# A hybrid decoder layer on one core: the mixer's first projection on x·g·(1 + scale), with the norm's roots multiplied into its sums

## The chip, the cores and the metric

The kernel runs on one core of a Trainium2 chip. The core has a matrix engine (TensorE, "PE" in the profile, with its weight loads as "PEld"), a vector engine (VectorE, "DVE"), an activation engine (ScalarE, "ACT"), a general engine (GpSimd, "POOL"), and a queue that issues transfers from device memory (SyncE, "SP"). Each engine runs its own instructions in order; they wait for each other through semaphores. The metric is the device time of one execution in microseconds, the median of several runs.

## The reference

One layer on x of 256 tokens by 2048 features: a feed-forward block at half weight, a token mixer, a second feed-forward block, a final norm. Ahead of each of the three blocks stands the same modulated norm, whose shift and scale (like the gate behind the block) come from a conditioning vector c.

```python
def rmsnorm(x, g):
    y = xf * lax.rsqrt(jnp.mean(xf * xf, axis=-1, keepdims=True) + EPS)
    return y * g
def ada_in(x, g, shift, scale):
    return rmsnorm(x, g) * (1.0 + scale[:, None, :]) + shift[:, None, :]

cond = jax.nn.silu(c)
mod = cond @ ada_w[l] + ada_b[l]          # 9 x 2048 values
sh1, sc1, gt1, sh2, sc2, gt2, sh3, sc3, gt3 = jnp.split(mod, 9, axis=-1)
h = ada_in(x, norm_g[l, 0], sh1, sc1)
x = x + 0.5 * gt1 * swiglu(h, w_gate0, w_up0, w_down0)
h = ada_in(x, norm_g[l, 1], sh2, sc2)
x = x + gt2 * hybrid_mixer(h, w_in, w_out, ...)
h = ada_in(x, norm_g[l, 2], sh3, sc3)
x = x + 0.5 * gt3 * swiglu(h, w_gate1, w_up1, w_down1)
return rmsnorm(x, final_norm)
```

`hybrid_mixer` projects h by `w_in` (queries, keys and values of 8 attention heads; queries, keys and values of 8 delta-rule heads behind a causal convolution of 4 taps and a silu; 24 gate columns; an output gate z), runs both groups of heads, and projects by `w_out`.

## The kernel before

**Layout.** Features lie on the 128 partitions, tokens along the free axis: x is 16 slices (index j or k, `KD` = 16) of 128 features by 256 tokens. A weight matrix is cut into tiles of 128 by 128; 5392 of them are packed in the order of use into 674 blocks of 8.

**Weights.** `Stream.next` (L124) hands out tiles. For each block it issues one transfer of 512 KB into a `wraw` tile (L119), ScalarE rounds it to `whi` (L121), VectorE makes the rest `wlo` = `wraw` - `whi` (L133). Four tiles of each kind exist (a few more of `wraw` in the feed-forward blocks), so a block's `whi` and `wlo` wait until TensorE has used the block four before. Activations are split the same way into `hs` HI and LO, and a product is hi·hi + hi·lo + lo·hi, three matrix instructions of 256 columns (L758 to L760 in the mixer), or one of 512 and one of 256 (L482, L483).

**Modulation columns.** The 144 columns of `mod` (9 parts of 16) are each a 1 MB transfer `adat` (L253) and one VectorE instruction over 2048 elements (L257). They are strewn between the weight blocks at the rate that `RATE` gives: from block 168 on 0.38 columns a block, from 264 on 0.1, from 280 on 0.25, from 408 on 0.125.

**Blocks by stage.** The first feed-forward block takes weight blocks 0 to 263; its last part, the down-projection of the second half, takes 232 to 263, two blocks for each of its 16 output slices j. The mixer's input projections are blocks 264 to 377, its output projection 378 to 409; the second feed-forward block is 410 to 673.

**Between the first feed-forward block and the mixer.** For each slice j of the down-projection, `residual` (L506, L507) adds to x on VectorE, `sumsq_add` squares on ScalarE (L306) and adds up on GpSimd (L310). Then `mixer` calls `modulate`: `norm_sums` (L320 on TensorE, L325 on ScalarE, L326 to L330 on VectorE) makes the inverse roots, `norm_row` (L338, L339) lays them out as a row over the tokens, and `modulate_one` makes h for one slice: x·g(1 + scale)·root (L365), plus shift and rounding to HI on ScalarE (L367, L368, L372), LO on VectorE (L369, L373). The projections begin with these h.

**The first projection** (`project`, L749) runs four outputs together, the slice k outside and the four inside: the gate columns ("gt") and the keys of heads 0 to 2; 8 blocks, 264 to 271. `gates` (L788) and `conv_silu` (L904) read its sums. Then come K3 to K7, single key heads of two blocks each, Z0 and V0 (z and attention values, 8 blocks each), and then G and F steps, which hold the heads' own work. `tick` advances that work (`gates`, `keys`, `solve`, `gdn`, `fox`) as the projections proceed; a scheduler then places each engine's instructions, and PSUM banks come from three pools of 3, 3 and 2.

**The second feed-forward block** begins in another way, by the class `Early`: `y(j)` writes x·g(1 + scale), without root and shift, into `hs` as soon as slice j of the output projection is done (L405 HI on ScalarE, L406 LO on VectorE), with the shift as one more column behind each half (258 columns at L421 and L423). `step(k)` makes the roots while the first products run, and the true h behind them; `scaled` (L427 to L430) multiplies the finished sums by the root row and takes out the shift's sum, which the reader adds as a bias.

Of the kernel before, what the change touches and what calls it, by code (L numbers as in the profile page):

```python
# [32 lines left out]

RATE = ((0, 0.5), (24, 0.34), (56, 0.45), (68, 0.06), (112, 0.5), (168, 0.38), (264, 0.1), (280, 0.25), (408, 0.125))
N_BIG, N_GDN = 3, 3
# [111 lines left out]
def layer_kernel(ctx: ExitStack, tc: tile.TileContext, xrow, c, adaw, cols, cst, w, out, order, dbg=None):  # L147
# [203 lines left out]

    plain = hsf[:, : KD * HS].rearrange("p (k i) -> p k i", k=KD)[:, :, : 2 * T].rearrange("p k (q t) -> p k q t", q=2)

    def part(k, q, extra=0):
# [5 lines left out]

    def modulate_one(j, g1, sh, r, weave=True):

        t = pt("ht")
        hl, hh, tt = (run(j, LO), run(j, HI), turns(t)) if weave else (plain[:, j, LO], plain[:, j, HI], t)
        V.scalar_tensor_tensor(t, x[:, j], g1, r, ALU.mult, ALU.mult)  # L365
        if j % 2:
            A.activation(t, t, AF.Identity, bias=sh)  # L367
            A.copy(hh, tt)  # L368
            return V.tensor_tensor(hl, tt, hh.bitcast(F32), ALU.subtract)  # L369
        else:  # L370
            with tc.issue_after(W.cast) if W.first else nullcontext():
                A.activation(hh, tt, AF.Identity, bias=sh)  # L372
            return V.scalar_tensor_tensor(hl, tt, sh, hh.bitcast(F32), ALU.add, ALU.subtract)  # L373
# [7 lines left out]

    def modulate(which, m_sh, m_sc):
        ada_need(max(m_sh, m_sc), KD - 1)
        g1 = gains(which, m_sc, 0, KD)
        r = norm_row(norm_sums())
        hq["next"], hq["one"] = 0, lambda j: modulate_one(
            j, g1[:, j : j + 1], mod[:, m_sh * KD + j : m_sh * KD + j + 1], r, False)

    class Early:

        def __init__(self, which, m_sh, m_sc):
            self.which, self.m_sh, self.m_sc, self.row, self.rstd = which, m_sh, m_sc, None, None

        def y(self, j):
# [7 lines left out]
            g = gains(self.which, self.m_sc, j, 1)  # L404
            A.activation(run(j, HI), turns(x[:, j]), AF.Copy, scale=g)  # L405
            V.scalar_tensor_tensor(run(j, LO), turns(x[:, j]), g, run(j, HI).bitcast(F32), ALU.mult, ALU.subtract)  # L406

        def step(self, k):
# [3 lines left out]
            if k == 4:  # L412
                self.row = norm_row(self.rstd, A.copy)
                g1 = gains(self.which, self.m_sc, 0, KD)
                hq["next"], hq["one"] = 0, lambda j: modulate_one(
                    j, g1[:, j : j + 1], mod[:, self.m_sh * KD + j : self.m_sh * KD + j + 1], self.row)
            if k > 4:
# [7 lines left out]
        def scaled(self, dst, ps):  # L425
# [3 lines left out]
            V.tensor_add(s[:, 1:], ps[:, T + 1 : T + 2], s[:, :1])  # L429
            V.tensor_tensor(dst, ps[:, :T], self.row, ALU.mult)  # L430
            return s[:, 1:]
# [180 lines left out]
    def ffn(which, m_gt, early=None):  # L612
        fs = list(range(NF))
        with tc.tile_pool(name=f"hid{which}", bufs=PARTS[which][1] + HIDX) as hp, \
                tc.tile_pool(name=f"more{which}", bufs=1) as more:
            W.more = more if MORE else None
            for half in range(2):
# [5 lines left out]
                for j in range(KD):  # L623
# [87 lines left out]
    early.close()  # L711
    norm2 = Early(2, 6, 7)
    if dbg is None or "ffn1" in dbg:
# [4 lines left out]
    def mixer():  # L718
        modulate(1, 3, 4)
        mx = ExitStack()  # L720
# [27 lines left out]

        def project(items):  # L749

            pp = [psn(i, "pp") for i in range(len(items))]
            todo = [(i, k) for k in range(KD) for i in range(len(items))]
            for i, k in todo:
                m, n = items[i]
                h_need(k)
                wh, wl = W.next(m, k, n)
                hh, hl = woven(plain[:, k, HI]), woven(plain[:, k, LO])
                PE.matmul(pp[i][:, :T], wh, hh, start=(k == 0), stop=False)  # L758
                PE.matmul(pp[i][:, :T], wh, hl, start=False, stop=False)  # L759
                PE.matmul(pp[i][:, :T], wl, hh, start=False, stop=(k == KD - 1))  # L760
                tick(TILE_US)
            return [p_[:, :T] for p_ in pp]

        def project_rows(mat, grp):

            pv = [psb("pv0"), psb("pv1")]
            for k in range(KD):
                wh, wl = W.next(mat, k, 4 * grp, 4)
                for t in range(2):
                    hh, hl = (plain[:, k, q, t * P : (t + 1) * P] for q in (HI, LO))  # L770
                    PE.matmul(pv[t], hh, wh, start=(k == 0), stop=False)
# [131 lines left out]

        def conv_silu(ps, n, dst):  # L904
# [4 lines left out]
            for s in range(1, 4):  # L909
                V.scalar_tensor_tensor(cv[:, s:], cp[:, : T - s], tap(3 - s), cv[:, s:], ALU.mult, ALU.add)  # L910
            A.activation(dst, cv, AF.Silu)
# [271 lines left out]

        def have_keys(h, ps):
            kk[h] = otile("kk")
            conv_silu(ps, NH + h, kk[h].bitcast(F32)[:, 0])
            if h % 4 == 0:
# [47 lines left out]
        W.late = True  # L1235
        first = project([("gt", 0)] + [("qkv", NH + h) for h in range(3)])
        start("k", -1, gates(first[0]))
        for h in range(3):
            have_keys(h, first[1 + h])
        for name in ORDER:  # L1240
# [183 lines left out]
```

## Time and profile before

| what | value |
|---|---|
| median of 3 runs | 1952.88 us (1949.29 to 1954.36) |
| the profiled execution | 1954.36 us |
| its span, first to last instruction | 1952.6 us |
| mean granted TensorE clock | 0.993 |
| weight and other transfers | 519.58 MB, mean 266 GB/s |

The profiled execution is the slowest of the three runs; its span is 1.8 us shorter than its device time. The page gives busy times by engine, the span in slices, the chain of waits that ended last, and groups of instructions by line; the trace gives every instruction in order of time. Matrix instructions are pipelined: one of 256 columns is shown with 0.28 us but the next one starts 0.11 us later, so the pace of TensorE is read from starts.

### The profile page before, as it was taken

What the parts mean: (1) busy time and instruction counts of PE and PEld (TensorE: products, weight loads), DVE (VectorE), ACT (ScalarE), POOL (GpSimd) and SP (SyncE); (2) the same over time, 40 slices, a digit from 0 to 9 for tenths busy, and PEclk for the clock granted to TensorE, in tenths of its full rate; (3) what the DMA queues carried; (4) which work ended last, traced back from release to release, by engine and by line L of the source; (5) the groups of instructions that cost most, each with busy time, mean ns of one, the idle gap of its engine ahead of it and who ended that gap; (6) DMA issues with size and microseconds to landing.
All of it is one profiled execution on the core that took longest, in us unless ns stands there. A gap on an engine that the chain in (4) does not pass through costs nothing.

```text
span 1952.6 us, 33709 instructions
## 1 busy us (share of the span) xinstructions
PE 1902.9 (97%) x13087; PEld 1776.3 (91%) x13087; DVE 1557.3 (80%) x2415; ACT 1035.5 (53%) x1645; POOL 57.0 (3%) x55
## 2 busy tenths in 40 slices
PE   8999999999999999999999999999999999999998
PEld 6999999998999988889989998889999999999997
DVE  6999978989999997889978979886766656565654
ACT  6544554433454446857657655565554445555553
POOL 0000000000000120000000002000000000000011
PEclk8999999999999999999999999999999999999999
DMA  9989867999999986685566658676777665555553
GB/s 369 359 321 349 300 221 254 398 381 376 356 353 342 347 317 218 251 302 205 203 239 236 211 215 315 226 258 249 255 249 239 201 200 203 201 200 202 200 202 119
DMA packets 129490, 519.58 MB, mean 266 GB/s; under 512 B 18217, under 2 KB 21545, under 8 KB 111153
## 3 DMA queue, kind: packets, MB, share of 16 engines
q1 hardware_dynamic: 129330, 517.42, 72.7%
q8 instruction: 103, 1.69, 0.3%
q14 instruction: 57, 0.47, 0.1%
HBM read 512.89 MB, written 4.47 MB: 265 GB/s over the span
## 4 chain that ended last, share of the span: by engine, by line
PE 76%; DVE 11%; DMA 5%; issue 4%; ACT 3%; SPq 0%; DVEq 0%; ACTq 0%
PE pd L482 14%; PE pg L478 10%; PE pu L478 10%; PE pd L483 7%; PE pu L479 5%; PE pg L479 5%; PE pgu L566 5%; PE pgu L565 5%; PE pgu L564 5%; DVE wlo L133 4%; DMA adat<-in_ada_dram 3%; DVE adat L257 2%; PE pp L758 2%; PE pp L759 2%; PE pp L760 2%
## 5 line engine op out<-in xcount | busy, mean ns | idle before, releaser
L133 DVE TENSOR_TENSOR wlo<-wraw,whi 128x1024 fp32r<-128x1024 f32 x674 | 821.1, 1227 | 242.7 <-ACT whi L121 241.3
L121 ACT CAST whi<-wraw 128x1024 fp32r<-128x1024 f32 x674 | 700.1, 1047 | 509.3 <-PE pd L482 166.5
L482 PE MATMUL pd<-hid,whi 128*128 128x512 f32 x1408 | 461.8, 382 | 0.0
L483 PE MATMUL pd<-hid,wlo 128*128 128x256 f32 x1408 | 384.6, 273 | 2.6 <-DVE wlo L133 2.4
L257 DVE CUSTOM_DVE_ANT_0 adat<-adat,cs,colt 128x2048 f32<-128x2048 f32 x140 | 329.5, 2354 | 40.9 <-DMA adat<-in_ada_dram 40.8
L478 PE MATMUL pg<-hs,whi 128*128 128x512 f32 x912 | 302.1, 382 | 2.5 <-DVE shc L429 2.5
L478 PE MATMUL pu<-hs,whi 128*128 128x512 f32 x912 | 302.2, 382 | 0.0
L482 PEld LDWEIGHTS pd<-hid,whi 128*128 128x128 f32 x1408 | 266.0, 189 | 36.5
L483 PEld LDWEIGHTS pd<-hid,wlo 128*128 128x128 f32 x1408 | 270.3, 192 | 5.4 <-DVE wlo L133 5.3
L564 PE MATMUL pgu<-hs,whi 128*128 128x256 f32 x896 | 245.3, 277 | 6.2 <-ACT hs L368 6.2
L479 PE MATMUL pu<-hs,wlo 128*128 128x256 f32 x912 | 249.3, 273 | 0.0
L479 PE MATMUL pg<-hs,wlo 128*128 128x256 f32 x912 | 248.9, 273 | 0.0
L566 PE MATMUL pgu<-hs,wlo 128*128 128x256 f32 x896 | 245.2, 278 | 2.4 <-DVE wlo L133 2.4
L565 PE MATMUL pgu<-hs,whi 128*128 128x256 f32 x896 | 246.8, 277 | 0.0
L478 PEld LDWEIGHTS pg<-hs,whi 128*128 128x128 f32 x912 | 172.4, 189 | 26.7 <-ACT whi L121 2.7
L478 PEld LDWEIGHTS pu<-hs,whi 128*128 128x128 f32 x912 | 172.4, 189 | 23.7
L758 PE MATMUL pp<-hs,whi 128*128 128x256 f32 x656 | 188.9, 289 | 1.5 <-ACT hs L372 1.5
L760 PE MATMUL pp<-hs,wlo 128*128 128x256 f32 x656 | 182.7, 278 | 1.1 <-DVE wlo L133 1.1
L759 PE MATMUL pp<-hs,whi 128*128 128x256 f32 x656 | 182.5, 278 | 0.0
L564 PEld LDWEIGHTS pgu<-hs,whi 128*128 128x128 f32 x896 | 172.3, 193 | 6.9 <-ACT hs L368 6.6
L479 PEld LDWEIGHTS pu<-hs,wlo 128*128 128x128 f32 x912 | 175.0, 192 | 1.3 <-DVE wlo L133 1.2
L479 PEld LDWEIGHTS pg<-hs,wlo 128*128 128x128 f32 x912 | 175.1, 192 | 0.4
(337 smaller groups left out, 2583.6 us busy)
## 6 DMA issues: line engine op xcount, KB each, us to landing
wraw<-in_w_dram SPq DMA_DIRECT2D x674, 512.0 KB, 4.3
adat<-in_ada_dram SPq DMA_DIRECT2D x140, 1024.0 KB, 7.4
xr<-in_xr_dram SPq DMA_DIRECT2D x4, 512.0 KB, 5.1
adaf<-in_ada_dram SPq DMA_DIRECT2D x4, 512.0 KB, 8.7
adaf<-in_ada_dram SPq DMA_DIRECT2D x2, 1024.0 KB, 11.3
xd<-x SPq DMA_DIRECT2D x4, 512.0 KB, 5.0
rw<-rowd SPq DMA_DIRECT2D x16, 128.0 KB, 6.7
x<-xd SPq DMA_DIRECT2D x4, 512.0 KB, 5.4
```

Of the source, the lines that this page charges most:

```text
L121: self.cast = self.nc.scalar.copy(self.h, r).ins
L133: nc.vector.tensor_tensor(self.l, r, self.h.bitcast(F32), ALU.subtract)
L257: V.tensor_tensor_reduce(t, t, cs, 1.0, L("adab", q, 1), ALU.mult, ALU.add, mod[:, q : q + 1])
L478: PE.matmul(ps, wt[0], both, start=(k == 0), stop=False)
L479: PE.matmul(ps[:, T:], wt[1], part(k, HI), start=False, stop=(k == KD - 1))
L482: PE.matmul(ps, wt[0], act.rearrange("p q (a b) -> p q b a", a=2), start=first, stop=False)
L483: PE.matmul(ps[:, :T], wt[1], woven(act[:, 0]), start=False, stop=last)
L564: PE.matmul(o, wh, part(k, HI), start=first and s == 0, stop=False, skip_group_check=skip)
L565: PE.matmul(o, wh, part(k, LO), start=False, stop=False, skip_group_check=skip)
L566: PE.matmul(o, wl, part(k, HI), start=False, stop=last, skip_group_check=skip)
L758: PE.matmul(pp[i][:, :T], wh, hh, start=(k == 0), stop=False)
L760: PE.matmul(pp[i][:, :T], wl, hh, start=False, stop=(k == KD - 1))
```

## The change

The mixer's first projection gets the treatment that the second feed-forward block has.

- `Early` takes a `view`, how the tokens of a slice are read: `turns` as so far, `runs` for the mixer. `norm1` is made for the mixer, and `norm1.y(j)` runs in the first feed-forward block's last down-projection behind each slice j. `modulate` is gone.
- The first `project` call gets `norm1`: 258, 256 and 258 columns on y; `early.step(k)` makes the roots at k = 2 and the root row at k = 4, and h for the later projections behind it. `conv_silu` of heads 0 to 2 and `gates` read their sums through `scaled`.
- `hs` keeps one layout, two halves of 128 tokens with 16 spare columns each, through the mixer; the matrix instructions read 256 columns in the same turn as before.
- `RATE` from block 232 on: 0.24, none from 264, 0.31 from 288, none from 404, 0.125 from 424.

```diff
-RATE = ((0, 0.5), (24, 0.34), (56, 0.45), (68, 0.06), (112, 0.5), (168, 0.38), (264, 0.1), (280, 0.25), (408, 0.125))
+RATE = ((0, 0.5), (24, 0.34), (56, 0.45), (68, 0.06), (112, 0.5), (168, 0.38), (232, 0.24), (264, 0.0), (288, 0.31), (404, 0.0), (424, 0.125))
...
-            A.activation(run(j, HI), turns(x[:, j]), AF.Copy, scale=g)
-            V.scalar_tensor_tensor(run(j, LO), turns(x[:, j]), g, run(j, HI).bitcast(F32), ALU.mult, ALU.subtract)
+            A.activation(run(j, HI), self.view(x[:, j]), AF.Copy, scale=g)
+            V.scalar_tensor_tensor(run(j, LO), self.view(x[:, j]), g, run(j, HI).bitcast(F32), ALU.mult, ALU.subtract)
...
-            V.tensor_tensor(dst, ps[:, :T], self.row, ALU.mult)
+            if self.view is turns:
+                V.tensor_tensor(dst, ps[:, :T], self.row, ALU.mult)
+            else:
+                V.tensor_tensor(runs(dst), turns(ps[:, :T]), runs(self.row), ALU.mult)
...
-                        if which == 1:
+                        if which == 0:
+                            norm1.y(j)
+                        else:
...
-    norm2 = Early(2, 6, 7)
+    norm1, norm2 = Early(1, 3, 4, runs), Early(2, 6, 7, turns)
...
     def mixer():
-        modulate(1, 3, 4)
...
-        def project(items):
+        def project(items, early=None):
...
+                if early is not None:
+                    if i == 0:
+                        early.step(k)
+                    early.products(pp[i], W.next(m, k, n), k)
+                    continue
...
+            if early is not None:
+                h_upto(KD)
+                return pp
...
-            A.copy(runs(yr[R]), turns(ps[R]))
+            d = pt("ey")
+            s = norm1.scaled(d, ps)
+            A.activation(yr[R], d[R], AF.Identity, bias=s[R])
...
-            A.copy(runs(cp), turns(ps))
+            if early is None:
+                A.copy(runs(cp), turns(ps))
+            else:
+                s = early.scaled(cp, ps)
+                A.activation(cp, cp, AF.Identity, bias=s)
...
-        first = project([("gt", 0)] + [("qkv", NH + h) for h in range(3)])
+        first = project([("gt", 0)] + [("qkv", NH + h) for h in range(3)], norm1)
```

The table of rates moves columns as follows, counted in the order of the transfers: 11 become 7 in blocks 232 to 263, 3 become none in 264 to 289, 29 become 36 in 290 to 404, 4 become none in 405 to 428, 10 become 14 behind.

**TensorE at the start of the mixer.** `pd_` are the sums of the last down-projection, `pp_` those of the first projection, one number for each bank in use. Before:

```order
L482 MATMUL pd_8153<-hid_7339,whi_8178 128x512
L483 MATMUL pd_8153<-hid_7339,wlo_8180 128x256
L320 MATMUL nsum_8209<-colt_87,sqacc_7394 128x2 x2
L320 MATMUL nsum_8209<-colt_87,sq_8202 128x2 x2
L339 MATMUL nrow_8224<-colt_87,rb_8223 128x128 x2
L758 MATMUL pp_8277<-hs_127,whi_8301 128x256
```

And now:

```order
L477 MATMUL pd_8203<-hid_7339,whi_8228 128x512
L478 MATMUL pd_8203<-hid_7339,wlo_8230 128x256
L413 MATMUL pp_8309<-hs_127,whi_8315 128x258
L414 MATMUL pp_8309<-hs_127,whi_8315 128x256
L415 MATMUL pp_8309<-hs_127,wlo_8317 128x258
L413 MATMUL pp_8310<-hs_127,whi_8315 128x258
```

The sums of squares (`nsum`) have moved behind the first block of products, 24 matrix instructions later, and the root row (`nrow`) into the third block; the products follow the down-projection directly.

**VectorE at the end of the first projection.** Before, where `cv_` is a convolution's sum and `ht_` a slice of h in the making:

```order
L369 TENSOR_TENSOR hs_127<-ht_8528,hs_127 128x256
L133 TENSOR_TENSOR wlo_8625<-wraw_8621,whi_8623 128x1024
L257 ISA adat_8627,mod_126<-adat_8627,cs_86,colt_87 128x2048
L257 ISA mod_126 128x1
L133 TENSOR_TENSOR wlo_8661<-wraw_8657,whi_8659 128x1024
L133 TENSOR_TENSOR wlo_8730<-wraw_8726,whi_8728 128x1024
L795 TENSOR_SCALAR coef_8639<-coef_8639 128x24
```

And now, where `pp_8310` and `pp_8311` are the sums of key heads 0 and 1, whose banks K3 and K4 take over:

```order
L363 SCALAR_TENSOR_TENSOR ht_8644<-x_85,g1_8395,nrow_8393 128x256
L133 TENSOR_TENSOR wlo_8693<-wraw_8689,whi_8691 128x1024
L367 TENSOR_TENSOR hs_127<-ht_8605,hs_127 128x2x128
L133 TENSOR_TENSOR wlo_8732<-wraw_8728,whi_8730 128x1024
L371 SCALAR_TENSOR_TENSOR hs_127<-ht_8628,mod_126,hs_127 128x2x128
L421 TENSOR_TENSOR shc_8652<-pp_8310,shc_8652 128x1
L425 TENSOR_TENSOR cp_8650<-pp_8310,nrow_8393 128x256
L421 TENSOR_TENSOR shc_8665<-pp_8311,shc_8665 128x1
```

The product of head 0's sums with the root row (L425), which releases the bank, stands on VectorE behind all but one of the instructions that make h and behind both blocks of K3; the modulation column has left. The gate columns' product comes three blocks of `wlo` behind this place.

**VectorE at the start of the second feed-forward block**, behind the root row's two instructions (L338). Before:

```order
L338 TENSOR_SCALAR rb_14473<-colt_87,nstd_14422 128x128 x2
L133 TENSOR_TENSOR wlo_14556<-wraw_14552,whi_14554 128x1024
L257 ISA adat_14666,mod_126<-adat_14666,cs_86,colt_87 128x2048
L257 ISA mod_126 128x1
L365 SCALAR_TENSOR_TENSOR ht_14507<-x_85,g1_14481,nrow_14479 128x256
```

And now:

```order
L338 TENSOR_SCALAR rb_14552<-colt_87,nstd_14501 128x128 x2
L133 TENSOR_TENSOR wlo_14635<-wraw_14631,whi_14633 128x1024
L133 TENSOR_TENSOR wlo_14674<-wraw_14670,whi_14672 128x1024
L363 SCALAR_TENSOR_TENSOR ht_14586<-x_85,g1_14560,nrow_14558 128x256
L363 SCALAR_TENSOR_TENSOR ht_14614<-x_85,g1_14560,nrow_14558 128x256
```

The modulation column between the root row and the making of h is gone, and one more block of weights stands there.

More of the change, by code (lines that the diff above doesn't have):

```diff
@@ L359, in run, with modulate_one @@
         return hs[:, k, q, :, :P]
-    def modulate_one(j, g1, sh, r, weave=True):
+    def modulate_one(j, g1, sh, r, view=turns):
         t = pt("ht")
-        hl, hh, tt = (run(j, LO), run(j, HI), turns(t)) if weave else (plain[:, j, LO], plain[:, j, HI], t)
+        hl, hh, tt = run(j, LO), run(j, HI), view(t)
         V.scalar_tensor_tensor(t, x[:, j], g1, r, ALU.mult, ALU.mult)
@@ L380, in gains, with __init__ @@
         return g1
[L382 to L387, printed above, removed]
     class Early:
-        def __init__(self, which, m_sh, m_sc):
+        def __init__(self, which, m_sh, m_sc, view):
             self.which, self.m_sh, self.m_sc, self.row, self.rstd = which, m_sh, m_sc, None, None
+            self.view = view
         def y(self, j):
@@ L415, in step @@
                 hq["next"], hq["one"] = 0, lambda j: modulate_one(
-                    j, g1[:, j : j + 1], mod[:, self.m_sh * KD + j : self.m_sh * KD + j + 1], self.row)
+                    j, g1[:, j : j + 1], mod[:, self.m_sh * KD + j : self.m_sh * KD + j + 1], self.row, self.view)
             if k > 4:
@@ L769, in project_rows @@
                 for t in range(2):
-                    hh, hl = (plain[:, k, q, t * P : (t + 1) * P] for q in (HI, LO))
+                    hh, hl = (hs[:, k, q, t, :P] for q in (HI, LO))
                     PE.matmul(pv[t], hh, wh, start=(k == 0), stop=False)
@@ L902, in mixer, with conv_silu @@
             G.memset(t_, 0.0)
-        def conv_silu(ps, n, dst):
+        def conv_silu(ps, n, dst, early=None):
             cp, cv = pt("cp"), pt("cv")
             tap = lambda s: L("conv", 4 * n + s, 1)
-            A.copy(runs(cp), turns(ps))
+            if early is None:
[3 more added lines that the diff above has]
+                A.activation(cp, cp, AF.Identity, bias=s)
             A.activation(cv, cp, AF.Copy, scale=tap(3))
-            for s in range(1, 4):
-                V.scalar_tensor_tensor(cv[:, s:], cp[:, : T - s], tap(3 - s), cv[:, s:], ALU.mult, ALU.add)
+            for d in range(1, 4):
+                V.scalar_tensor_tensor(cv[:, d:], cp[:, : T - d], tap(3 - d), cv[:, d:], ALU.mult, ALU.add)
             A.activation(dst, cv, AF.Silu)
@@ L1235, in mixer @@
         W.late = True
-        first = project([("gt", 0)] + [("qkv", NH + h) for h in range(3)])
+        first = project([("gt", 0)] + [("qkv", NH + h) for h in range(3)], norm1)
         start("k", -1, gates(first[0]))
         for h in range(3):
-            have_keys(h, first[1 + h])
+            have_keys(h, first[1 + h], norm1)
         for name in ORDER:
```

7 lines of the change are left out of this document (3 added, 4 removed).

## Prediction

> **What bounds the kernel now.** I read the page's totals and chain first, then busy times by stage (the windows view), then each engine's timeline at the edited places.
>
> ```profile
> span 1952.6 us, 33709 instructions
> PE 1902.9 (97%) x13087; PEld 1776.3 (91%) x13087; DVE 1557.3 (80%) x2415; ACT 1035.5 (53%) x1645; POOL 57.0 (3%) x55
> PE 76%; DVE 11%; DMA 5%; issue 4%; ACT 3%; SPq 0%; DVEq 0%; ACTq 0%
> ```
>
> TensorE sets the end: it is busy for 97%, and only 49.7 us are its holes. The change removes no large product, so it can save only holes, a low clock, or waits. Windows (start:end and length; busy time with count for PE, PEld, DVE, ACT, POOL; granted clock; DMA share; GB/s):
>
> ```profile
> 660.00:742.00 82.00, 81.07 (x493) 73.87 (x491) 74.25 (x95) 37.70 (x49) 21.83 (x15) 1.00 0.84 318
> 742.00:748.00 6.00, 1.66 (x10) 1.35 (x10) 5.46 (x15) 2.26 (x6) 1.07 (x5) 0.86 0.53 184
> 748.00:754.00 6.00, 6.00 (x33) 6.00 (x33) 5.22 (x12) 3.12 (x8) 0.42 (x2) 0.57 0.20 78
> 858.00:872.00 14.00, 9.98 (x83) 9.23 (x81) 12.43 (x20) 13.91 (x34) 0.43 (x2) 1.00 0.96 339
> 872.00:1000.00 128.00, 122.23 (x982) 116.38 (x981) 113.85 (x329) 84.34 (x208) 0.00 (x0) 1.00 0.59 205
> 1000.00:1050.00 50.00, 49.60 (x330) 46.02 (x330) 38.48 (x50) 29.35 (x42) 0.00 (x0) 1.00 0.81 298
> 1050.00:1150.00 100.00, 96.85 (x827) 93.83 (x826) 86.06 (x220) 64.78 (x155) 0.00 (x0) 1.00 0.55 198
> 1277.00:1280.00 3.00, 0.47 (x4) 0.47 (x4) 3.00 (x10) 2.18 (x8) 0.00 (x0) 1.00 1.00 403
> ```
>
> Four places matter: the step into the mixer (742 to 754: 4.34 us idle, then granted clock 0.57); the down-projection ahead of it, where VectorE is busy for 91% of the time; the mixer from 858 on, where TensorE loses 4.02 + 5.77 + 0.40 + 3.15 = 13.3 us; and the start of the second feed-forward block (2.53 us idle at 1277).
>
> **A, the step into the mixer.** TensorE's rows before (start, duration, instruction, in brackets what it waited for):
>
> ```profile
> 741.42 0.27 PE L483 MATMUL pd<-hid,wlo 128*128 128x256 f32 x1
> 741.53 0.51 PE L320 MATMUL nsum<-colt,sqacc 128*128 128x2 f32 x4
> 747.69 1.23 PE L758 MATMUL pp<-hs,whi 128*128 128x256 f32 x4 [1.55 <-ACT hs L372]
> 752.54 0.42 PE L759 MATMUL pp<-hs,whi 128*128 128x256 f32 x1
> 752.76 0.42 PE L760 MATMUL pp<-hs,wlo 128*128 128x256 f32 x1
> 771.73 0.28 PE L760 MATMUL pp<-hs,wlo 128*128 128x256 f32 x1
> 771.84 0.28 PE L758 MATMUL pp<-hs,whi 128*128 128x256 f32 x1
> ```
>
> Call 741.53 t0. The first product comes 6.2 us later, at half pace (0.22 from start to start where 0.11 is usual), and K3 begins at 771.84, t0 + 30.3. VectorE's rows there:
>
> ```profile
> 742.25 0.48 DVE L507 SCALAR_TENSOR_TENSOR x<-pd,gh,x 128x256 f32<-128x256 f32 x1
> 746.62 1.26 DVE L365 SCALAR_TENSOR_TENSOR ht<-x,g,nrow 128x256 f32<-128x256 f32 x3
> 748.59 0.48 DVE L373 SCALAR_TENSOR_TENSOR hs<-ht,mod,hs 128x256 fp32r<-128x256 f32 x1
> 748.98 0.41 DVE L369 TENSOR_TENSOR hs<-ht,hs 128x256 fp32r<-128x256 f32 x1
> 749.32 0.47 DVE L365 SCALAR_TENSOR_TENSOR ht<-x,g,nrow 128x256 f32<-128x256 f32 x1
> 766.56 0.41 DVE L369 TENSOR_TENSOR hs<-ht,hs 128x256 fp32r<-128x256 f32 x1
> ```
>
> In the changed order products follow t0 directly. TensorE's own work up to K3 is 192 products x 0.112 = 21.5 us, plus about 0.5 for the last slice's residual (VectorE is busy with it until 742.73), 1.0 for `nsum` (two instructions of 0.51), 1.1 for `nrow` and its wait: t0 + 24.1. But K3 takes head 0's bank, and the instruction that releases it (L425) stands on VectorE behind nearly all of h. VectorE, step by step:
> - residual until t0 + 1.2, the last LO of y, then `wlo` of block 268. Its `whi` tile is free when TensorE is through block 264 (0.5 + 24 x 0.112 = 3.2), the cast takes 1.05, `wlo` 1.2: t0 + 5.5.
> - the roots: their sums come behind block 264, then some five small instructions, which I put at 0.2 each, and the row: t0 + 7.3; `wlo` 269 and its tail, t0 + 8.8.
> - 31 instructions of h at 0.34 to 0.39 from start to start (rows at 748.59 to 749.32) and a few a little more, 12.0; four more `wlo` at 1.13, 4.5; L421 and L425, 0.5; waits for ScalarE, 0.4. Together t0 + 26.2.
>
> ```profile
> 857.15 1.05 ACT L121 CAST whi<-wraw 128x1024 fp32r<-128x1024 f32 x1 [7.90 <-DMA wraw<-in_w_dram]
> 683.11 1.21 DVE L133 TENSOR_TENSOR wlo<-wraw,whi 128x1024 fp32r<-128x1024 f32 x1
> 684.24 0.47 DVE L507 SCALAR_TENSOR_TENSOR x<-pd,gh,x 128x256 f32<-128x256 f32 x1
> ```
>
> So K3 starts 30.3 - 26.2 = 4.1 us earlier. Queued behind L425 on VectorE are the products for heads 1 and 2 and the gates; where TensorE's next instruction waits for the gates' sums, about 8 us behind K3's start, I allow 0.5. **A = -3.6.** Bounds: t0 + 24.1 if VectorE is never late (-6.2); t0 + 30 if its stretch of h takes as long as before, 746.62 to 766.97 with five `wlo` in it (-0.3). I stay near the middle, since the counts are known and only waits are not. The low clock goes with the hole: K3's wait of about 2 us is shorter than the 2.53 at 1277, where the clock stayed at 1.00.
>
> **B, the down-projection ahead.** Its 11 columns become 7, and 16 times y comes in.
>
> ```profile
> 741.20 0.38 PE L482 MATMUL pd<-hid,whi 128*128 128x512 f32 x1
> 685.76 0.14 DVE L504 TENSOR_SCALAR gh<-mod 128x1 f32<-128x1 f32 x1
> 768.03 2.35 DVE L257 CUSTOM_DVE_ANT_0 adat<-adat,cs,colt 128x2048 f32<-128x2048 f32 x1
> L133 DVE TENSOR_TENSOR wlo<-wraw,whi 128x1024 fp32r<-128x1024 f32 x36 | 46.5, 1302 | 1.9 <-ACT whi L121 1.7
> L406 DVE SCALAR_TENSOR_TENSOR hs<-x,g,hs x16: 478/962/1002, 1177.5 to 1247.6; 128x256 fp32r<-128x256 f32 x16
> 691.17 1.07 POOL L310 TENSOR_TENSOR sqacc<-sqacc,sq 128x256 f32<-128x256 f32 x1 [4.74 <-ACT sq L306]
> ```
>
> The L406 row gives shortest, median and longest of the same y in the other block: 0.96 as a rule, beside GpSimd's addition of squares, 0.48 alone. For each slice VectorE then has 2 `wlo` x 1.14, 2 residuals x 0.40, small ones 0.19, y 0.92 (a few alone), and 7/16 of a column, 1.03: 5.22 us. TensorE has 16 pairs x 0.33 (L482 to L483 and on): 5.2. They are level, and TensorE lost 0.93 here before. Four columns less (-9.4) stand against 16 y (+14.7), so VectorE goes to about 81 of 82 us. Where two engines are level, each wait of VectorE's costs; I take **B = +1.0**. Bounds: -0.9 (the old loss vanishes) and +10 (each y as long as two of these in turn, third rival).
>
> **C, the second feed-forward block's start.** There a column and its wait leave:
>
> ```profile
> 1254.62 2.35 DVE L257 CUSTOM_DVE_ANT_0 adat<-adat,cs,colt 128x2048 f32<-128x2048 f32 x1 [2.60 <-DMA adat<-in_ada_dram]
> 1278.91 0.15 DVE L429 TENSOR_TENSOR shc<-pg,shc 128x1 f32<-128x1 f32 x1
> 1279.54 0.45 PE L478 MATMUL pg<-hs,whi 128*128 128x512 f32 x1 [2.53 <-DVE shc L429]
> ```
>
> VectorE gains up to 4.95 us, of which one block of `wlo`, moved ahead, only changes place. TensorE waits 2.53 at the end for L429 and L430, which stand behind h. What is left is ScalarE's copy, L429 and L430, about 1.0: **C = -1.5**, between -2.5 (nothing left) and -0.5 (h stays bound by ScalarE).
>
> **D, the mixer's columns.** Seven more in blocks 290 to 404, three fewer in 264 to 289.
>
> ```profile
> PE pd L483 <- DVE wlo L133: 0.9, 3, 0.3
> DVE adat L257 <- DMA adat<-in_ada_dram: 14.0, 10, 2.7
> ```
>
> (Total us, number of waits, longest.) VectorE waits 14.0 us for some 34 columns between 760 and 1260, 0.41 each, and TensorE's 13.3 us of holes there say that about half reaches it: 7 x 0.2 = +1.4, less 0.2 for the three that go; **D = +1.2**. Below: 0, as VectorE has 14 us of room in 872 to 1000; above: 2.8. The four columns added behind block 424 lie in the second feed-forward block beside dense products; I cost them at nothing, and at 0.41 each, 1.6, if that cover is gone. The other layout of `hs` costs nothing: reading 256 columns in turns or straight starts every 0.11 us.
>
> **Sum:** -3.6 + 1.0 - 1.5 + 1.2 = -2.9. The profiled execution took 1954.36 (its span 1952.6 and 1.76 around it), so 1951.5; it was 1.48 above the median of its runs, so a median of **1950.0**.
>
> **The rivals.**
> *Faster: VectorE keeps up everywhere.* A -6.2 (L425 in time), B -0.9, C -2.5, D +0.7: -8.9, 1944. For it: every wait that I charge is at a place where the engines are within 2 us of each other. Against: L425 stands where it stands, and 31 instructions of h must be ahead of it.
>
> *The gain is given back in the mixer.* The gates' product comes three blocks of `wlo` behind L425, so the decays and the first head's solve start some two blocks, 5 us, later against the projections that cover them; 858 to 872 lost 4.0 already, with GpSimd idle and ScalarE busy for 99%. If that hole grows by 3 to 4 us, the sum is about 0 to +1: 1953.5. For it, too: in the changed order head 0's solution is written two blocks later (303, not 301), and the delta rule's first step, which reads it, stays at TensorE's block 304. Against: one block is still between them, and VectorE is not full there.
>
> *Slower: VectorE and GpSimd in each other's way in the down-projection.* The place is `y` beside L310:
>
> ```profile
> 679.51 2.19 POOL L310 TENSOR_TENSOR sqacc<-sqacc,sq 128x256 f32<-128x256 f32 x1 [3.79 <-ACT sq L306]
> 681.11 1.68 DVE L133 TENSOR_TENSOR wlo<-wraw,whi 128x1024 fp32r<-128x1024 f32 x1
> ```
>
> The addition takes 1.07 alone and 2.19 where it meets VectorE, and the `wlo` that it meets takes 1.68, not 1.21. If each LO of y waits a whole addition, it takes 0.48 + 1.07 = 1.55 and a slice 5.85: 16 x 0.63 = 10 over TensorE's pace, 11 with B's 1.0, a total of +7.1: 1960. It decides from 4 us lost there on (then A, C and D are eaten). Against: the median of 0.96 in the other block, where y meets the same addition. The Trainium skill ("SBUF — State Buffer", section "Who interferes with whom") says that the two engines share a port pair under an exclusive lock held for the whole instruction, the loser blocked; a lock met at its start would give this 1.55, an estimate. The longest L406, 1.00, does not show it; the 2.19 of the addition does.
>
> **How the numbers follow.** About 0.3%, 5.9 us, is what a measurement of this kernel can tell from no change: faster is below 1947.0, slower above 1958.7. Chances: my forecast 0.35 (0.30 within, 0.05 faster, for its own range is 1946 to 1954); the faster rival 0.30, all faster; given back 0.15 (0.13 within, 0.02 slower); the collision 0.18 (0.03 within, 0.15 slower); 0.02 for a clock that stays low at K3's wait (748 to 754 cost 2.6) with the collision, slower. Together faster 0.35, same 0.46, slower 0.19. The range, 1943.5 to 1957.5, holds all of the first three and the collision's mild end; it leaves out its hard end and a gain beyond 9 us.
>
> **What would show it.** Right: products right behind the last `pd`, clock 1.00, no hole of 4 us; K3's first product waits about 2 us for `cp` (L425); `y` LO (L398) at a median near 0.96, and TensorE's waits for `wlo` in the down-projection at 1 to 3 us in all; the wait for `shc` in the second feed-forward block near 1.0; a little more idle time from 858 on. Wrong: K3 at t0 + 24 with no wait (faster rival), a hole from 858 to 872 of 7 us or more (given back), or L398 near 1.5 with TensorE waiting in each slice (collision). A step that I have not seen would be a new wait at the gates' sums above 2 us.

## The result, and the profile after

The changed kernel takes 1946.51 us (median of 10 runs, 1941.67 to 1950.73), the kernel before 1952.5 us (10 runs, 1948.43 to 1954.96): ratio 0.997, 95% interval 0.9957 to 0.9983. It is 6.0 us faster; 2.9 were forecast, and 1946.5 lies inside the range. The profiled execution took 1947.07 us, 7.29 less than the one shown of before.

The totals of the page:

```profile
span 1945.3 us, 33788 instructions
PE 1901.1 (98%) x13087; PEld 1776.4 (91%) x13087; DVE 1565.4 (80%) x2456; ACT 1045.1 (54%) x1666; POOL 55.0 (3%) x55
```

VectorE has 8 us more work and the end comes 7.3 us earlier: what changed is where TensorE waits. Busy time by stage, in the columns of the prediction:

```profile
657.87:739.60 81.73, 81.73 (x501) 75.11 (x500) 79.94 (x120) 45.70 (x65) 15.99 (x14) 1.00 0.82 291
765.40:769.00 3.60, 3.53 (x18) 3.56 (x19) 3.60 (x9) 2.34 (x7) 0.00 (x0) 0.55 0.80 257
858.00:872.00 14.00, 12.87 (x110) 12.28 (x110) 12.13 (x31) 11.60 (x33) 0.42 (x2) 1.00 0.78 277
872.00:1000.00 128.00, 124.38 (x960) 117.46 (x959) 119.12 (x327) 84.99 (x199) 0.00 (x0) 1.00 0.68 240
1000.00:1050.00 50.00, 46.44 (x327) 44.37 (x327) 36.14 (x49) 24.95 (x40) 0.00 (x0) 0.93 0.74 275
```

The down-projection (first row) has no hole at all, though VectorE is busy for 98% of it. From 858 to 872 TensorE loses 1.13 us where it lost 4.02. But 1000 to 1050, where it had lost 0.40, now loses 3.56, and the granted clock falls to 0.93.

TensorE's start of the mixer:

```profile
739.53 0.27 PE L478 MATMUL pd<-hid,wlo 128*128 128x256 f32 x1
739.64 0.28 PE L413 MATMUL pp<-hs,whi 128*128 128x258 f32 x1
762.51 0.28 PE L415 MATMUL pp<-hs,wlo 128*128 128x258 f32 x1
765.47 0.55 PE L759 MATMUL pp<-hs,whi 128*128 128x256 f32 x1 [2.69 <-DVE shc L421]
765.82 0.42 PE L760 MATMUL pp<-hs,whi 128*128 128x256 f32 x1
```

The products follow the down-projection 0.11 us behind its last one. K3 starts at t0 + 25.8 (t0 is now 739.64) after a wait of 2.69. The row names L421, the first of the two instructions on VectorE that read head 0's sums; L425, the second, ends at 765.32, right before K3. VectorE there:

```profile
748.45 1.27 DVE L363 SCALAR_TENSOR_TENSOR ht<-x,g,nrow 128x256 f32<-128x256 f32 x3
764.84 0.16 DVE L421 TENSOR_TENSOR shc<-pp,shc 128x1 f32<-128x1 f32 x1
764.90 0.42 DVE L425 TENSOR_TENSOR cp<-pp,nrow 128x256 f32<-128x256 f32 x1
```

To see where the time went, take the same matrix instruction by its number in both traces (both have 13087) at the borders of the stages, and subtract. The other traces lack one record in the first 25 us, so their instructions are counted from the end. The second profile of the changed kernel is the first experiment below. The last column is the last experiment: behind the down-projection its engines run the changed kernel's instructions in the same order, so in A, D and C it is a third execution of the same code.

| stage (times of before) | forecast | changed | changed, second profile | last experiment |
|---|---|---|---|---|
| start to 674 | 0 | -0.1 | -0.8 | -0.7 |
| B: 674 to 741, the last down-projection | +1.0 | -1.7 | -1.7 | -1.7 |
| A: 741 to 777, the step into the mixer | -3.6 | -3.1 | -4.6 | -4.6 |
| D: 777 to 1234, the mixer | +1.2 | +3.3 | +7.3 | -0.9 |
| C: 1234 to 1340, around the second block's start | -1.5 | -5.5 | -3.9 | -2.4 |
| 1340 to the end | 0 | 0.0 | 0.0 | 0.0 |
| sum | -2.9 | -7.3 | -3.7 | -10.4 |

### The profile page after: what moved, and what is told of

It reads as the page before. It is cut to its first block, busy times and chain, and to the rows that moved or that the text cites. A ratio compares the mean times of both kernels' runs of the same rounds, so it can differ in the third digit from the quotient of the medians.

```text
span 1945.3 us, 33788 instructions
## 1 busy us (share of the span) xinstructions
PE 1901.1 (98%) x13087; PEld 1776.4 (91%) x13087; DVE 1565.4 (80%) x2456; ACT 1045.1 (54%) x1666; POOL 55.0 (3%) x55
## 5 line engine op out<-in xcount | busy, mean ns | idle before, releaser
L559 PEld LDWEIGHTS pgu<-hs,whi 128*128 128x128 f32 x896 | 172.4, 194 | 7.3 <-ACT hs L366 6.9
L759 PE MATMUL pp<-hs,whi 128*128 128x256 f32 x592 | 172.2, 291 | 2.7 <-DVE shc L421 2.7
L561 PEld LDWEIGHTS pgu<-hs,wlo 128*128 128x128 f32 x896 | 171.6, 193 | 3.3 <-DVE wlo L133 3.3
L560 PEld LDWEIGHTS pgu<-hs,whi 128*128 128x128 f32 x896 | 173.1, 193 | 0.0
```

Of the source, the lines that this page charges most:

```text
L559: PE.matmul(o, wh, part(k, HI), start=first and s == 0, stop=False, skip_group_check=skip)
L560: PE.matmul(o, wh, part(k, LO), start=False, stop=False, skip_group_check=skip)
L561: PE.matmul(o, wl, part(k, HI), start=False, stop=last, skip_group_check=skip)
```

## The experiments

All stage figures below are worked out like those of this table, against the same profile of before; each is of one profiled execution, the ratios are of several.

### The changed kernel once more

No edit.

> The changed kernel once more, for a second profile. If the holes of the mixer are set by the order of the instructions (place decides), they stand at the same instructions with about the same lengths: 2 to 4 us at the product of the convolution's result near 1036, 0.8 to 1.5 us at wlo near 1178. If they are chance of the transfers, they differ by more than half from one execution to the next, and the readings of single profiles by stage do not hold.

One execution, 1950.72 us. The holes stand at the same instructions: 5.01 us where 3.56 stood, 1.46 and 0.46 for `wlo` where 1.34 and 0.46 stood. Two of its TensorE rows:

```profile
764.82 0.35 PE L759 MATMUL pp<-hs,whi 128*128 128x256 f32 x1 [2.69 <-DVE shc L421]
1038.28 0.47 PE L1014 MATMUL pvq<-colt,qv 128*128 128x128 f32 x1 [5.01 <-ACT qv L921]
```

So the order of the instructions sets the places, but not the sizes: in the last experiment, with the same order, the hole of 3.56 and 5.01 is 1.15. One profile gives stage D (+3.3, +7.3, -0.9) to about 4 us either way, A and C to about 1.5, and B, where no transfer decides, to 0.1.

### The table of rates alone

```diff
 before.py
-RATE = (... (168, 0.38), (264, 0.1), (280, 0.25), (408, 0.125))
+RATE = (... (168, 0.38), (232, 0.24), (264, 0.0), (288, 0.31), (404, 0.0), (424, 0.125))
```

> The kernel before with the new table of rates and nothing else. Theory 1 (columns and early products both pay): the down-projection loses its 0.93 us of waits, the stretch from the output projection's end to the second feed-forward block's start gains about 5, the mixer gives back 1 to 3; the 6.2 us between the last down-projection product and the mixer's first product stay as they were. Total -2 to -5 us, ratio 0.9975 to 0.999. Theory 2 (the early products carry the gain, the table only makes room for them): within 1 us of the kernel before, ratio 0.9995 to 1.001.

1960.78 us, ratio 1.0046 (1.0028 to 1.0064): slower, which neither theory had. B -1.7, A +0.3, C -3.7 are near what theory 1 said, but the mixer lost 18 us. (The profiled execution, 1968.18, is the slowest of its runs and 7 us above their median; if those 7 us lie in the mixer too, it lost 11 at the median.) The largest hole is the one that the changed kernel has at 1036, here 5.29. VectorE's rows ahead of it:

```profile
1044.02 0.48 DVE L910 SCALAR_TENSOR_TENSOR cv<-cp,colt,cv 128x255 f32<-128x255 f32 x1
1049.36 2.35 DVE L257 CUSTOM_DVE_ANT_0 adat<-adat,cs,colt 128x2048 f32<-128x2048 f32 x1 [4.87 <-DMA adat<-in_ada_dram]
1051.64 0.48 DVE L910 SCALAR_TENSOR_TENSOR cv<-cp,colt,cv 128x254 f32<-128x254 f32 x1
1053.17 0.48 DVE L910 SCALAR_TENSOR_TENSOR cv<-cp,colt,cv 128x253 f32<-128x253 f32 x1
```

A column stands between the first and the second tap of a convolution. VectorE takes its instructions in order, so the convolution waits 4.87 us for a transfer that it has no use for and 2.35 for the column. ScalarE's silu makes `qv` of that convolution, and TensorE waits for `qv`. The changed kernel has the same, on VectorE and then on TensorE:

```profile
1027.84 0.48 DVE L920 SCALAR_TENSOR_TENSOR cv<-cp,colt,cv 128x255 f32<-128x255 f32 x1
1031.23 2.35 DVE L257 CUSTOM_DVE_ANT_0 adat<-adat,cs,colt 128x2048 f32<-128x2048 f32 x1 [2.91 <-DMA adat<-in_ada_dram]
1033.51 0.48 DVE L920 SCALAR_TENSOR_TENSOR cv<-cp,colt,cv 128x254 f32<-128x254 f32 x1
1035.04 0.48 DVE L920 SCALAR_TENSOR_TENSOR cv<-cp,colt,cv 128x253 f32<-128x253 f32 x1
```

```profile
1036.08 0.48 PE L1014 MATMUL pvq<-colt,qv 128*128 128x128 f32 x1 [3.56 <-ACT qv L921]
```

The hole follows the column's wait. In the second profile of the changed kernel the column waits 4.68 where TensorE then waits 5.01; in the last experiment 0.82, and TensorE 1.15:

```profile
1033.43 2.35 DVE L257 CUSTOM_DVE_ANT_0 adat<-adat,cs,colt 128x2048 f32<-128x2048 f32 x1 [4.68 <-DMA adat<-in_ada_dram]
```

```profile
1026.93 2.35 DVE L257 CUSTOM_DVE_ANT_0 adat<-adat,cs,colt 128x2048 f32<-128x2048 f32 x1 [0.82 <-DMA adat<-in_ada_dram]
```

```profile
1031.78 0.33 PE L1014 MATMUL pvq<-colt,qv 128*128 128x128 f32 x1 [1.15 <-ACT qv L921]
```

With K3 in another bank and with the mixer's columns earlier (both below), where the column stands at the same place, it is 3.29 and 4.04, and 1.67 and 2.00. In these six profiles TensorE waits 0.3 to 0.8 us longer than the column does; most of the column's own 2.35 us is covered.

### The early products alone

```diff
 after.py
-RATE = (... (168, 0.38), (232, 0.24), (264, 0.0), (288, 0.31), (404, 0.0), (424, 0.125))
+RATE = (... (168, 0.38), (264, 0.1), (280, 0.25), (408, 0.125))
```

> The changed kernel with the old table of rates. Theory 1 (the table is what lets y lie beside the down-projection): VectorE has 0.76 instead of 0.44 columns for each slice, 5.2 + 0.75 = 5.97 us against TensorE's 5.23, so TensorE waits for wlo, 8 to 12 us in the down-projection; the step into the mixer still gains 3, the second block's start is as before; total +5 to +9, ratio 1.0025 to 1.0045. Theory 2 (VectorE's lead of four blocks swallows y): the down-projection loses 2 us or less and the total is -2 to -4, ratio 0.998 to 0.999.

1955.88 us, ratio 1.0012 (1.0001 to 1.0024). B +5.3, A -3.2, D -1.2, C +1.8. At 0.38 y is not hidden; TensorE's waits in the last down-projection (total us, number, longest):

```profile
PE pd L478 <- DVE wlo L133: 2.8, 3, 0.9
PE pd L478 <- DVE gh L499: 2.2, 3, 0.8
```

Six waits, where the changed kernel has none. Against B at 0.24 (-1.7) the 4 columns more cost 7.0 us, 1.8 each. Theory 1 had expected 8 to 12 us in the down-projection and a ratio of 1.0025 or more, theory 2 at most 2 us and a gain: the result lies between them. Neither half of the change is a gain alone: the table makes the room for y, and costs in the mixer about what y's early products earn.

### The columns around the second block's start

```diff
 before.py
-(280, 0.25), (408, 0.125))
+(280, 0.25), (404, 0.0), (424, 0.125))
```

> The kernel before with one change in its table: no columns in blocks 404 to 423, 0.125 behind. Theory 1 (all four columns of that stretch cost): TensorE's wait of 2.38 us for wlo at the end of the output projection and most of the 2.53 at the second feed-forward block's start go, -5 us, ratio 0.9975. Theory 2 (as predicted, only the column at the start counts): -1.5 us, ratio 0.999 to 1.000, and the wait at the end of the output projection stays above 1.5 us.

1948.91 us, ratio 0.998 (0.997 to 0.999), -4 us; stage C -3.2. The wait of 2.38 for `wlo` at 1239 is gone; the one for `shc` at the block's start shrank from 2.53 to 1.88. This one piece of the table is about two thirds of the whole change's gain, with nothing done to the projection. Up to 1219 us this kernel's engines run the instructions of before in the same order, and yet its profile shows -3.8 in stage D and +2.5 from 67 to 674: so far two executions of the same code differ, those of before too.

### K3 in another bank

```diff
 after.py
-pp = [psn(i, "pp") for i in range(len(items))]
+pp = [psn(bank + i, "pp") for i in range(len(items))]
...
-have_keys(h, project([("qkv", NH + h)])[0])
+have_keys(h, project([("qkv", NH + h)], bank=4 if h == 3 else 0)[0])
```

> The changed kernel, with the sums of K3 in a bank of the second pool, so that they do not wait for head 0's product with the root row. Theory 1 (that product alone holds K3, and the half clock behind it comes from the hole): K3 starts at about t0 + 23.2 with a wait under 0.6 us, the clock stays at 1.00, 4 us less than the changed kernel, ratio to the kernel before about 0.995. Theory 2 (VectorE as a whole is late, the hole only moves): K3 starts early, but wlo, K4 or the gates' column sums wait 2 us or more behind it, and the total stays at the changed kernel's, ratio 0.997.

1952.28 us, ratio 1.000 (0.9987 to 1.0013). The ratio is above what both theories gave (0.995 and 0.997). Stage A is -7.2, so head 0's product was what held K3: it starts without a wait. Of the 4 us, 1.65 come back at once at the gates' column sums (TensorE's rows):

```profile
775.64 0.30 PE L806 MATMUL pcol<-colt,x 24*128 24x24 f32 x2 [1.65 <-ACT x L797]
1042.24 0.47 PE L1014 MATMUL pvq<-colt,qv 128*128 128x128 f32 x1 [4.04 <-ACT qv L921]
```

The mixer lost 11.3. Much of that is the same hole (4.04 here) and waits for `wlo`; whether the bank or the columns' new neighbours made them, this run does not tell.

### The mixer's columns three blocks earlier

```diff
 after.py
-(288, 0.31), (404, 0.0)
+(285, 0.31), (401, 0.0)
```

> The changed kernel with the mixer's columns three blocks earlier (0.31 from 285, none from 401); their number stays. Theory 1 (place decides): the holes move, the mixer from 772 to 1233 changes by 3 us or more either way against the changed kernel's +3.2, ratio anywhere from 0.993 to 1.001 but not 0.997. Theory 2 (number decides): the same +3 there, ratio 0.997 within 0.001.

1951.45 us, ratio 0.9985 (0.9974 to 0.9995); D +7.3, A -4.6, C -3.5. The hole at `pvq` shrank to 2.00, and new ones came (1.45 for `wlo` at 860, 1.19 for `whi` at 858). D lies within what the same code shows without the shift (-0.9 to +7.3), so this run does not separate place from number.

### Seven of the mixer's columns elsewhere, and both together

First into blocks 168 to 231 ("ahead"), without and with K3's bank as above:

```diff
 after.py
-(68, 0.06), (112, 0.5), (168, 0.38), (232, 0.24), (264, 0.0), (288, 0.31)
+(68, 0.06), (112, 0.5), (168, 0.49), (232, 0.24), (264, 0.0), (288, 0.25)
```

> The changed kernel with seven columns of the mixer (0.25 a block from 288, not 0.31) moved into blocks 168 to 231 (0.49, not 0.38). Theory 1 (a column costs by where it stands between the chain's instructions; at 0.31 one stands, behind a late transfer, inside the convolution whose result the delta rule waits for): the 3.56 us hole at 1036 and the 2.1 of half clock behind it go, 5 to 8 us less than the changed kernel, ratio 0.993 to 0.9945. Theory 2 (as predicted, each column costs about 0.2 of TensorE's time): -1.4, ratio 0.9965. Theory 3 (blocks 168 to 231 are full, transfers there late): TensorE loses 3 us or more in that stretch, ratio 0.998 or more.

> K3 in a bank of the second pool and the seven columns moved ahead, together. Theory 1 (the second pool's bank is a gain of 4 us at K3 of which the gates' column sums take 2.3 back, and the rest of its loss came from where columns stood): 1 to 3 us less than with the columns alone, ratio 0.992 to 0.994. Theory 2 (K3 earlier only brings the wait for the gates and, at 850 to 875, for the first heads' keys): the same as with the columns alone or up to 3 us more.

Then into blocks 68 to 111 ("early"), without and with the bank:

```diff
 after.py
-(68, 0.06), (112, 0.5), (168, 0.38), (232, 0.24), (264, 0.0), (288, 0.31)
+(68, 0.22), (112, 0.5), (168, 0.38), (232, 0.24), (264, 0.0), (288, 0.25)
```

> The changed kernel with the mixer at 0.25 a block, not 0.31, and its seven columns in blocks 68 to 111 (0.22, not 0.06), where the DMA share is 0.62 to 0.69 and VectorE is busy for 76 to 88%, not in 168 to 231, where they cost 11 us. Theory 1 (that place has room): nothing is lost up to the mixer, and the mixer keeps the 3.2 us gained with the columns moved ahead: 4 to 7 us less than the changed kernel, ratio 0.993 to 0.995. Theory 2 (VectorE's queue is full there too, a column delays wlo): TensorE loses 3 us or more in blocks 68 to 111, ratio 0.997 or more.

> The same seven columns in blocks 68 to 111, and K3 in a bank of the second pool. Theory 1 (the 11 us of the columns in 168 to 231 were the only loss of that pair): TensorE's holes from 670 to 1300 stay near 11 us, the total is 15 us or more below the kernel before, ratio 0.990 to 0.993. Theory 2 (K3's bank is worth nothing): as with the columns alone, 0.993 to 0.995.

And into blocks 68 to 97 alone ("front"), with the bank:

```diff
 after.py
-(68, 0.06), (112, 0.5), (168, 0.38), (232, 0.24), (264, 0.0), (288, 0.31)
+(68, 0.323), (98, 0.0), (112, 0.5), (168, 0.38), (232, 0.24), (264, 0.0), (288, 0.25)
```

> K3 in the second pool's bank and the seven columns in blocks 68 to 97 alone (0.323, then none up to 111), since in the run with them up to 111 TensorE's waits for wlo stood from 309 on (4.7 of 6 us). Theory 1 (the last blocks before the down-projection are the full ones): the 6 us lost before the down-projection become 2 or less, the rest stays: 4 us less than that run, ratio 0.992. Theory 2 (VectorE is full over the whole stretch, only its lead hides it at first): the loss moves to 220 to 300 and stays at 5 us or more, ratio 0.994 to 0.995.

The third column of figures is the stretch from 67 to 674 us, in which the changed kernel has +0.9 and 0.0.

| run | median us | ratio (95%) | 67 to 674 | A | D | C |
|---|---|---|---|---|---|---|
| ahead | 1950.55 | 0.9987 (0.9975 to 0.9999) | +11.9 | -4.6 | -3.2 | -5.5 |
| ahead, K3's bank | 1946.92 | 0.9967 (0.9955 to 0.9979) | +11.9 | -7.2 | -5.4 | -6.3 |
| early | 1944.45 | 0.9966 (0.9954 to 0.9978) | +7.4 | -3.0 | -6.5 | -6.3 |
| early, K3's bank | 1940.20 | 0.9942 (0.993 to 0.9954) | +8.5 | -7.2 | -6.4 | -6.3 |
| front, K3's bank | **1934.80** | 0.9915 (0.9901 to 0.9929) | +2.5 | -7.2 | -6.7 | -6.3 |

B is -1.7 in all five. With seven columns fewer and K3 in its old bank, stage D is -3.2 and -6.5, where the changed kernel has +3.3, +7.3 and -0.9: 2 to 14 us less, 8 between the means, or 1.2 a column against 0.2 forecast. With K3's new bank it goes from +11.3 to between -5.4 and -6.7. Place and number of the columns change together here. Fewer columns do not rule such a hole out: "ahead" has one of 3.53 us at 879, and the early products alone, also at 0.25 a block, one of 3.59 at 880, both at the same product (L1014) of an earlier head. What they cost elsewhere depends on the place. In blocks 168 to 231 it is all that the mixer gained and more (theory 3 of that run), so both "ahead" runs miss the ratio of their theory 1; the window of the changed kernel from 600 to 658 has no idle time, here 5.34 us. "Ahead" in that window, and TensorE's waits for `wlo` from 480 to 680:

```profile
600.00:658.00 58.00, 52.66 (x316) 47.35 (x315) 49.76 (x58) 25.70 (x39) 0.00 (x0) 1.00 0.89 351
```

```profile
PE pu L474 <- DVE wlo L133: 7.1, 4, 1.8
```

In blocks 68 to 111 it is 7.4 and 8.5, so those two runs missed their expected ratios although the mixer did as theory 1 said. In blocks 68 to 97 it is 2.5, no more than two executions of the same code differ there. TensorE's waits from 220 to 345 with K3's bank, columns to 111 first, then to 97:

```profile
PE pgu L561 <- DVE wlo L133: 5.1, 5, 1.8
PE pd L478 <- DVE wlo L133: 0.9, 1, 0.9
```

```profile
PE pgu L561 <- DVE wlo L133: 1.0, 1, 1.0
PE pgu L559 <- ACT whi L121: 0.6, 1, 0.6
```

Theory 1 of the last run holds: the last blocks before the down-projection were the full ones. K3's bank, no gain with 0.31 in the mixer (1.000 against 0.997), is worth about 4 us (0.9987 to 0.9967, 0.9966 to 0.9942) once the columns are out of the way. The place at 1036 in the last run, VectorE's rows:

```profile
1026.35 2.35 DVE L257 CUSTOM_DVE_ANT_0 adat<-adat,cs,colt 128x2048 f32<-128x2048 f32 x1 [0.71 <-DMA adat<-in_ada_dram]
1028.97 0.48 DVE L920 SCALAR_TENSOR_TENSOR cv<-cp,colt,cv 128x255 f32<-128x255 f32 x1
1030.50 0.48 DVE L920 SCALAR_TENSOR_TENSOR cv<-cp,colt,cv 128x254 f32<-128x254 f32 x1
```

The column stands ahead of the convolution and waits 0.71, and TensorE loses 0.60 there. The wait is short as well, so this row alone does not show what the place is worth. This version, 17 us below the kernel before, beats both kernels.

### The sum of squares on VectorE

```diff
 after.py
-            G.tensor_tensor(sqa["acc"], sqa["acc"], s, ALU.add)
+            (V if not W.late else G).tensor_tensor(sqa["acc"], sqa["acc"], s, ALU.add)
```

> The changed kernel with the first feed-forward block's sum of squares added up on VectorE in place of GpSimd. Theory 1 (y's LO takes 0.96 us because it meets GpSimd's addition): its median falls to 0.48, VectorE's busy time in the down-projection stays within 1 us of the changed kernel's 79.9 (16 x 0.48 saved, 15 x 0.42 added). Theory 2 (the operands make it slow, two inputs and a rounding): the median stays at 0.96.

One execution, 1944.33 us. y's LO in the last down-projection (shortest, median, longest in ns), in the changed kernel and here, where 15 of the 16 lie in the window shown:

```profile
L398 DVE SCALAR_TENSOR_TENSOR hs<-x,g,hs x16: 473/958/965, 665.7 to 742.0; 128x256 fp32r<-128x256 f32 x16
```

```profile
L398 DVE SCALAR_TENSOR_TENSOR hs<-x,g,hs x15: 472/477/501, 665.2 to 736.6; 128x256 fp32r<-128x256 f32 x15
```

GpSimd's addition is what doubles y, by 0.48 us. One of these meetings in the changed kernel, GpSimd's row and VectorE's:

```profile
690.78 1.07 POOL L310 TENSOR_TENSOR sqacc<-sqacc,sq 128x256 f32<-128x256 f32 x1 [2.04 <-ACT sq L306]
```

```profile
691.18 0.96 DVE L398 SCALAR_TENSOR_TENSOR hs<-x,g,hs 128x256 fp32r<-128x256 f32 x1
```

In all 13 meetings y begins 0.4 to 0.65 us behind the addition's start and ends 0.28 behind its end; the three y that meet none take 0.48. VectorE is busy for 77.55 of 81.56 us, 2.4 less than with GpSimd's help, where at most 1 was expected. Stage B is -1.7 as in the changed kernel: there was nothing left to gain.

## Why the prediction was right, and where it was wrong

The direction and the range were right; the forecast time was 3 us too high, and its terms erred in both directions. In the first profile A took 0.5 and D 2.1 us more than forecast, B 2.7 and C 4.0 less: that the sum stayed in the range is in part luck.

**A was right.** The forecast had the first h at t0 + 8.8 and K3 at t0 + 26.2, held by L425; measured are 8.8 (748.45) and 25.8, with that wait 2.69 for "about 2". K3's bank shows that L425 was the holder. "The low clock goes with the hole" held in some executions: in the first profile the clock fell once more behind K3's wait (0.55), in the second it did not, hence -3.1 and -4.6 around the forecast -3.6.

**B had the wrong sign** (+1.0 for -1.7, beyond the bound of -0.9). VectorE's load was well sized: the prediction's own numbers, 74.25 - 9.4 + 14.7, give 79.6 us (its "about 81" is 1.4 too much), and 79.9 was measured. What failed is "Where two engines are level, each wait of VectorE's costs". The waits of before came from 0.38 columns a block, and went with them in every run at 0.24, with y or without; y added no wait of TensorE's. The bound of -0.9 counted the waits of the matrix instructions only; what three waits cost is 1.7, read from starts.

**C was mis-sized** (-1.5 for -5.5, -3.9 and -2.4; its bound was -2.5). The change empties blocks 405 to 428 of four columns, and the step priced one of them, the one at 1254. TensorE's wait for `wlo` at 1239, in the trace of before, had no term:

```profile
1239.49 0.38 PE L483 MATMUL po<-oh,wlo 128*128 128x256 f32 x1 [2.38 <-DVE wlo L133]
```

The run with this piece alone has no such wait, -3.2 in that stage and a ratio of 0.998.

**D was priced the wrong way** (+1.2 for +3.3, +7.3 and -0.9). The three executions leave room for the forecast itself, but not for its price of 0.2 a column: seven columns less were worth some 8 us in the mixer, not 1.4. The average of 0.41 us of VectorE's waits for each column, half of it taken as TensorE's, hides that few columns wait (in the changed kernel five waits make 12.3 us from 760 to 1235), and that one of these stands inside a chain and hands its whole wait on. Cut finer and counted from the start of D, the changed mixer is 6.7, 3.8 and 6.5 us ahead of before by 1000 (times of before, the three executions in turn), loses 5.7, 6.6 and 0.6 from there to 1050, where the convolution's hole stands, and 4.3, 4.5 and 5.0 from 1050 to 1234. The run "early", with seven columns less, gains in all three stretches: 2.9, 0.1 and 3.5. So that one hole makes most of the difference between executions, while the last loss repeats; TensorE's waits at L1188 belong to it (3.1 to 3.4 us in all, 0.4 in "early"), and what makes them was not tried. The sum in D has a slip too: at 0.2 each the three columns that go are worth 0.6, not 0.2, so D should have been +0.8.

**The rivals.** "The gain is given back in the mixer" was right in the stage for two of the three executions and wrong in the mechanism: 858 to 872 lost less than before, the gates cost under 1 us, and the hole that gave back most in both profiles of the changed kernel came from a column in one of the delta rule's convolutions. The 6.0 us gained lie midway between the forecast's 2.9 and the faster rival's 8.9: B and C went that rival's way, but K3 did wait. The collision is there, as sized at 0.96, and cost nothing; no LO of y waited a whole addition (the longest took 0.965, not 1.55). The Trainium skill ("SBUF — State Buffer", section "Who interferes with whom") has a VectorE instruction with two SBUF inputs contend with a GpSimd instruction that reads SBUF; the two rows of L398 agree. The loss was 0.48 us, less than the whole 1.07 of the addition; but y began 0.4 us or more into the addition and ended behind its end, so the rows do not rule out that y waits for that end.

**Open:** why the same table costs the kernel before 18 us in the mixer (11 at its median, if the profile's excess lies there) and the changed one between -1 and +7; and whether the place of a column or the lateness of its transfer is what seven columns fewer improve. The scheduler orders the two differently throughout the mixer; which of these differences counts was not tried.

## What to carry to other kernels

An instruction that waits for its own transfer should not be priced by an average on an in-order engine: find the instruction behind it and who waits for that one. In six profiles a column inside a convolution handed its whole wait on to TensorE; what a place ahead of the chain would save was not measured apart. When a change brings work to a stage and takes other work out of it, run each half alone: here the table alone was slower (1.0046), the early products alone brought nothing (1.0012), and together they were faster. K3's earlier start (stage A shorter by 2.6 to 4.1 us) showed in the time only in the runs that had seven columns fewer in the mixer. Before a stage is read from one profile, profile the same code again: here the mixer differed by 8 us between three executions.

## What the runs showed of the hardware

A hole's length does not settle whether the clock falls. The same wait of 2.69 us ahead of K3 was followed by a granted clock of 0.55 in the first profile of the changed kernel and of 1.00 in the second; a wait of 1.88 us in the run with the start's columns moved was followed by 0.66, where before 2.53 at that place left it at 1.00. Rows of the second profile of the changed kernel, then of that run:

```profile
764.80:768.40 3.60, 3.58 (x32) 3.60 (x33) 3.60 (x9) 2.34 (x7) 0.00 (x0) 1.00 0.79 240
```

```profile
1272.50:1276.00 3.50, 3.46 (x14) 3.03 (x15) 3.50 (x12) 2.21 (x4) 0.00 (x0) 0.66 0.04 8
```

In stage A the difference is 1.5 us for one and the same code. The Trainium skill ("TensorE: Matmul & The Clock Gate", section "What's actually happening") has the monitor's window running freely, whatever the kernel does; that fits a hole that counts in one execution and not in the next.
